# One transformer block in float32 on one core: where VectorE makes the weight sums of the up projection, who scales the keys, and how the first gate's row is made

## The chip, the cores and the metric

The kernel runs on one core of one Trainium2 chip. The metric is the device time of one execution in microseconds (us). Before the change the median of three runs was 2684.64 us (2683.98 to 2686.53).

## The reference

One block of a network on 512 tokens of width D = 2048, with 256 context tokens, all in float32:

```python
sh1, sc1, g1, sh2, sc2, g2 = split(silu(c) @ w_ada + b_ada, 6)      # the same for the context
px = modulate(x, sh1, sc1) @ w_in                                   # q, v, two forget gates, g, pool, conv
pc = modulate(ctx, csh1, csc1) @ w_in[:, :4 * 1024]
_, s_f, s_b = hgrn2_bidir(pc, ...)                                  # states left by the context
ox, _, _ = hgrn2_bidir(px, ..., s_f, s_b, True)                     # 8 heads of 128, forward and backward
yx = concatenate([ox, local_mixers(px[..., 5120:])], -1) @ w_out
x = layer_norm(ALPHA * x + g1 * yx, ln1_g, ln1_b)
u, g = split(modulate(x, sh2, sc2) @ w_up, 2)                       # 2 x 5632 columns
x = layer_norm(ALPHA * x + g2 * ((u * silu(dwconv3(g))) @ w_down), ln2_g, ln2_b)
```

`hgrn2_bidir` is a gated linear attention: each token's key and value enter a state that a forget gate shrinks, once in each direction.

## The kernel before

**Products.** TensorE works on a rounded float32 format. Each operand is therefore split into a high part (a cast, on ScalarE) and a low part (the value less its high part, on VectorE), and each product is three matmuls: high by high, high by low, low by high (`mm3`, lines L111, L112, L113 in turn; tiles named `h` or `H` are high, `l` or `L` low). `wload` (L95 to L106) does this for a streamed weight: a transfer on SyncE's queue into `wr`, the cast (L105), the subtraction (L106), with three buffers for the raw tile and two for each part.

**Stages.** The ramp (`ada_first`, `modulate1`, `ramp`) computes the first modulation, transposes the normalised tokens and the context (`hxh`/`hxl` at L310/L311, `hch`/`hcl` at L329/L330), and projects the context and the first heads. It lasts to about 391 us. Then `pair`, `conv` and `pool` project the tokens on all columns of `w_in`, to about 1024 us. Between two weight tiles of a projection they call `background()` (L645), which steps two generators of the linear attention (`gla`, L551, one for each of two heads) and three steps of `ada_rest` (L658), which streams the rest of `w_ada` and sums it on VectorE (`aacc`, L680 and L682).

A `gla` generator does one level of a binary tree over the tokens at each step (`LEVELS` = 1 to 64): it copies keys (`kc`, ScalarE, L562), multiplies keys by queries on TensorE (`lv`, L566), puts the masked result into `A` (VectorE, L641), scales the queries (`Q`, VectorE, L582) and the keys (`K`, two GpSimd operations, L585 and L586), and multiplies the decays (`T`, VectorE, L587). At the first level it also adds the keys of both directions (`kd`, GpSimd, L572) for the diagonal (`dg`, TensorE).

From 1024 to 1225 us `out_half` (L815) multiplies by `w_out`, once for each half of the tokens, in four blocks `j` of 512 columns, each from eight weight tiles. `norm_mid` (L846) does the layer norms behind it and transposes the tokens for the feed-forward part (`x2T`). The gate g1 lies as a column over the partitions (`mods2`), but is needed as a row on all partitions: `row_prepare` (L708) makes four diagonal matrices (`dg`, L715), their high part `dh` (L718) and low part `dl` (L719); `row_chunk` (L722) multiplies each by a matrix of ones (`row_g`, L726 and L727) and copies the result (`rowt_g`, L729). The product with the gate is L840 (`wt`).

**The up projection.** Two pairs of column groups are done plainly (`up_half`). The other twenty (`up_pair`, L1032; from 1333.62 to about 2176 us) use the seven-product scheme of Strassen and Winograd on 2 x 2 blocks (`combine`, `up_block`). One call of `weights7` (L977), a block here, loads four tiles of 128 rows by four column tiles into `W` (SyncE, L989), makes the three further factors of the scheme by sums on VectorE (L992, L993, L994: 128 x 1024, 128 x 512 and 128 x 512 elements), and has `parts` (L968) split it in two units: cast `H` (L973) and low part `L` (L974), each 128 x 1792. A unit feeds 42 matmuls of 256 columns, a block 84. A pair has a gate `g` and a value `u`, each of two blocks (`_0` and `_1`), so there are 80 blocks. After a gate's or value's last block VectorE adds up the products (`Z`, L1026 to L1029) and does the convolution and the gating (`cv`, L936, L938, L1042, L1047).

**What sets the order.** The engines run their queues in order. A scheduler places what the program traces, by priority: weights are traced under `high_priority(offset=AHEAD)`, so that they are placed ahead of the work around them, as far as data and buffers allow. There are three buffers of `W` (two in `ww`, one in `w3`), and three each of `H` and `L`. So the transfer into a block's `W` waits until the last low part of the block three before has been made, and a unit's cast waits until TensorE has used the unit three before.

**The rest.** `down` (L1104, about 2176 to 2627 us) multiplies by `w_down`; `finish` does the last layer norm.

Of the kernel before, what the change touches and what calls it, by code (L numbers as in the profile page):

```python
# [16 lines left out]
P = 128  # L17
# [55 lines left out]
class Kernel:  # L73
# [35 lines left out]
    def mm3(self, out, st, mv, start, stop):  # L109
        mm = self.nc.tensor.matmul  # L110
        mm(out=out, lhsT=st[0], rhs=mv[0], start=start, stop=False)  # L111
        mm(out=out, lhsT=st[0], rhs=mv[1], start=False, stop=False)  # L112
        mm(out=out, lhsT=st[1], rhs=mv[0], start=False, stop=stop)  # L113
# [21 lines left out]
    def setup(self):  # L135
        nc, I, pp = self.nc, self.I, self.persist
        self.ident = pp.tile([P, P], F32, name="ident")
        make_identity(nc, self.ident)
        self.ones = pp.tile([P, 32], F32, name="ones")
        nc.vector.memset(self.ones, 1.0)  # L140
        self.ones_r = pp.tile([P, P], F32R, name="ones_r")
        nc.scalar.copy(out=self.ones_r, in_=vw(self.ones[:, :], [[0, 4], [1, 32]]))
        self.mhalf = pp.tile([P, 4], F32, name="mhalf")
        nc.vector.memset(self.mhalf, -0.5)
        self.zero = pp.tile([P, 1], F32, name="zero")
        nc.vector.memset(self.zero, 0.0)
        self.cols = {}
# [149 lines left out]
    def modulate1(self, xp, rp, k0, n):  # L297

        nc = self.nc
        m = lambda k, i: self.mods1[:, 4 * k + i:4 * k + i + 1]  # L300
        tmp = xp.tile([P, n, L], F32, name=f"tx_{k0}", tag="v", bufs=2)
        for e in range(n):
            k = k0 + e
            fs = slice((k % 4) * P, (k % 4 + 1) * P)
            pt = self.glbank(f"xT_{k}")
            for t in range(NTT):
                nc.tensor.transpose(out=pt[:, t * P:(t + 1) * P], in_=self.xn[t][k // 4][:, fs], identity=self.ident)
            nc.vector.tensor_scalar(out=tmp[:, e], in0=pt, scalar1=m(k, 2), scalar2=m(k, 0), op0=ALU.mult, op1=ALU.add)
            h, l = self.a2(f"hxh_{k}"), self.a2(f"hxl_{k}")
            nc.scalar.copy(out=h, in_=tmp[:, e])  # L310
            (nc.vector if k0 < 2 else nc.gpsimd).tensor_tensor(out=l, in0=tmp[:, e], in1=h.bitcast(F32), op=ALU.subtract)  # L311
            self.hxh.append(h)
            self.hxl.append(l)

    def modulate1_ctx(self, rp, k0, n):
# [14 lines left out]
        nc.gpsimd.tensor_tensor(out=l, in0=tmp, in1=h.bitcast(F32), op=ALU.subtract)  # L330
# [5 lines left out]
    def proj_T(self, banks, wt, kts, hi, lo, first, last, shared=False):  # L336

        wh, wl = wt
        for j, k in enumerate(kts):
            for h in range(2):  # L340
                self.mm3(banks[h], (wh[:, j, h * P:(h + 1) * P], wl[:, j, h * P:(h + 1) * P]),
                         (hi[k], lo[k]),
                         start=(first and j == 0 and (h == 0 or not shared)),
                         stop=(last and j == len(kts) - 1 and (h == 1 or not shared)))

    def proj_N(self, banks, wt, kts, hi, lo, ntt, first, last):

        wh, wl = wt
        for j, k in enumerate(kts):
            for t in range(ntt):  # L350
                tk = slice(t * P, (t + 1) * P)
                self.mm3(banks[t // 2][:, (t % 2) * 256:(t % 2) * 256 + 256],
                         (hi[k][:, tk], lo[k][:, tk]), (wh[:, j, :], wl[:, j, :]),
                         start=(first and j == 0 and t % 2 == 0),
                         stop=(last and j == len(kts) - 1 and t % 2 == 1))
# [195 lines left out]
    def gla(self, gp, hd, q, Q, K, T, V, gs):  # L551
# [7 lines left out]
        for li, m in enumerate(LEVELS):  # L559
# [8 lines left out]
            if li == 0:  # L568
# [3 lines left out]
                nc.gpsimd.tensor_tensor(out=kd, in0=K[:, 0], in1=K[:, 1], op=ALU.add)  # L572
# [10 lines left out]
            kf = vw(Ka, [[2 * m, nb], [1, m]])  # L583
            kb = vw(Ka, [[2 * m, nb], [1, m]], L + m)
            nc.gpsimd.tensor_tensor(out=kf, in0=kf, in1=vw(cur, [[2, nb], [0, m]], ts_ + 1), op=ALU.mult)  # L585
            nc.gpsimd.tensor_tensor(out=kb, in0=kb, in1=vw(cur, [[2, nb], [0, m]]), op=ALU.mult)  # L586
# [58 lines left out]
    def background(self):  # L645
# [3 lines left out]
        if self.steps:  # L649
            next(self.steps[0], None)  # L650
            if n < len(LEVELS) or n >= len(LEVELS) + TAIL_LAG:
                next(self.steps[1], None)
# [54 lines left out]

    def row_prepare(self, name, base, j, dg=None):  # L708

        nc = self.nc  # L710
        if dg is None:
            dg = self.a2(f"dg_{name}_{j}", F32)
        dh, dl = self.a2(f"dh_{name}_{j}"), self.a2(f"dl_{name}_{j}")
        for i in range(4):
            nc.vector.tensor_scalar(out=dg[:, i * P:(i + 1) * P], in0=self.ident,  # L715
                                    scalar1=self.mods2[:, base + 4 * j + i:base + 4 * j + i + 1], scalar2=None,
                                    op0=ALU.mult)
        nc.scalar.copy(out=dh, in_=dg)  # L718
        nc.vector.tensor_tensor(out=dl, in0=dg, in1=dh.bitcast(F32), op=ALU.subtract)  # L719
        return dh, dl  # L720

    def row_chunk(self, pool, name, j, parts, tag):  # L722

        nc = self.nc
        pb = self.glbank(f"row_{name}_{j}")
        nc.tensor.matmul(out=pb, lhsT=self.ones_r, rhs=parts[0], start=True, stop=False)  # L726
        nc.tensor.matmul(out=pb, lhsT=self.ones_r, rhs=parts[1], start=False, stop=True)  # L727
        t = pool.tile([P, 512], F32, name=f"rowt_{name}_{j}", tag=tag[0], bufs=tag[1])
        nc.scalar.copy(out=t, in_=pb)  # L729
        return t  # L730
# [84 lines left out]
    def out_half(self, cp, hf):  # L815
# [8 lines left out]
        for j in range(4):  # L824
            b = [self.mmbank(f"wo_{hf}_{j}_{i}") for i in range(2)]
            for q in range(8):
                if q == 4:
                    parts = self.row_prepare(f"g1_{hf}", 0, j,
                                             cp.tile([P, 512], F32, name=f"dg_{hf}_{j}", tag="rc", bufs=2))
# [7 lines left out]
            g1 = self.row_chunk(cp, f"g1_{hf}", j, parts, ("rb", 1))  # L837
# [130 lines left out]
    def parts(self, ww, name, src, n):  # L968
# [5 lines left out]
        nc.vector.tensor_tensor(out=Lw[:, 0:n], in0=src, in1=H[:, 0:n].bitcast(F32), op=ALU.subtract)  # L974
        return H, Lw

    def weights7(self, ww, name, src, c0):  # L977
# [6 lines left out]
        with self.tc.high_priority(offset=AHEAD):  # L984
# [7 lines left out]
            tt(out=pair(4, 3), in0=pair(3, 1), in1=pair(2, 3), op=ALU.subtract)  # L992
            tt(out=W[:, :, 5], in0=W[:, :, 1], in1=W[:, :, 4], op=ALU.subtract)  # L993
            tt(out=W[:, :, 6], in0=W[:, :, 0], in1=W[:, :, 5], op=ALU.subtract)  # L994
            units = []
            for c in range(0, NB, NU):
                units += self.parts(ww, f"{name}_{c}", W[:, c:c + NU].rearrange("p a s m -> p (a s m)"), 7 * NU * P),
        return units
# [179 lines left out]
    def run(self):  # L1178
# [5 lines left out]
        self.y_d = [self.dram.tile([P, 4, 512], F32, name=f"y_d{t}") for t in range(NTT)]  # L1184
        self.g2_d = self.dram.tile([1, D], F32, name="g2_d")
        self.y, self.h2, self.S, self.h = {}, ({}, {}), {}, {}
        self.upc = self.wcount = 0
        with tc.tile_pool(name="wts", bufs=1, reuse_waits="tile", side="right") as self.wts:
# [77 lines left out]
```

## Time and profile before

| | |
|---|---|
| median of three runs | 2684.64 us |
| profiled execution, its own time | 2687.12 us |
| its span | 2685.3 us |
| mean granted TensorE clock | 0.985 |
| busy: TensorE, VectorE, ScalarE, GpSimd | 2545.6, 1897.1, 928.8, 256.1 us |
| up projection | 1333.62 to about 2176 us |

The profile is of one execution. The span reaches from its first to its last instruction, and the execution's own time is 1.8 us longer. Busy times are shares of that span; an average over the stages says little, since the ramp, the projections, the up and the down projection have different limits. A row of a group names line, engine, operation, the tile written and the tiles read, the count, the busy time in us and the mean of one in ns, and then the idle time of the engine just ahead, with what ended it. A wait's row has the total in us, the count and the longest. A row of the timeline has start and length in us, and in brackets the idle time before it.

### The profile page before, as it was taken

To read this page: it belongs to the slowest core of one execution; us is meant where nothing else is said; L and a number is where in the kernel's file an instruction comes from. 1 tells how busy PE (TensorE), PEld (TensorE's weight loads), DVE (VectorE), ACT (ScalarE), POOL (GpSimd) and SP (SyncE) were. 2 spreads that over 40 slices of the span, in tenths; PEclk is the share of its full clock that TensorE was granted. 3 is DMA by queue.
4 is the path that set the end of the run, shared out by engine and by line. 5 is a ranking of instruction groups with operands and counts; after the bars stand their busy time and mean duration, and the time that the engine had idled before them with its cause. 6 is when DMAs were issued, how large, how long until landed. Compare 5 with 4: busy or idle time off the path is not lost.

```text
span 2685.3 us, 40002 instructions
## 1 busy us (share of the span) xinstructions
PE 2545.6 (95%) x16332; PEld 2240.9 (83%) x16332; DVE 1897.1 (71%) x2408; ACT 928.8 (35%) x1119; POOL 256.1 (10%) x255
## 2 busy tenths in 40 slices
PE   5999999999999999999899999999999899999996
PEld 4677998888878888769899999999999888888885
DVE  5543569968698866778988889888898864433338
ACT  5221254232333324354543334433343342222111
POOL 0120102213051300001100000000000000000005
PEclk9999999999999999999999999999999999999998
DMA  8755236756646546657533333333333374333321
GB/s 266 235 181 164 87 95 224 235 167 197 204 148 209 160 128 207 209 188 243 160 111 120 109 110 118 111 107 117 116 104 125 103 247 155 127 122 131 109 94 63
DMA packets 301461, 409.85 MB, mean 153 GB/s; under 512 B 17669, under 2 KB 193117, under 8 KB 300765
## 3 DMA queue, kind: packets, MB, share of 16 engines
q1 hardware_dynamic: 297692, 395.76, 45.8%
q0 software_dynamic: 3584, 11.54, 1.1%
q8 instruction: 128, 2.10, 0.4%
q14 instruction: 57, 0.46, 0.1%
HBM read 387.30 MB, written 19.93 MB: 152 GB/s over the span
## 4 chain that ended last, share of the span: by engine, by line
PE 55%; DVE 19%; DMA 15%; issue 6%; ACT 2%; POOL 1%; SPq 1%; DVEq 0%; POOLq 0%; ACTq 0%
DMA W_g<-in_w_up_dram 7%; DMA W_u<-in_w_up_dram 6%; PE dn L113 6%; PE dn L112 6%; PE dn L111 5%; DVE L_g L974 3%; DVE L_u L974 3%; DVE W_u L992 2%; PE wo L112 2%; PE wo L113 2%; PE wo L111 1%; PE rx L111 1%; PE rc L111 1%; PE rx L113 1%; PE rc L112 1%
## 5 line engine op out<-in xcount | busy, mean ns | idle before, releaser
L974 DVE TENSOR_TENSOR L_dn<-W_dn,H_dn 128x1536 fp32r<-128x1536 f32 (+1 forms) x56 | 96.2, 1719 | 223.2 <-ACT H_dn L973 223.2
L973 ACT CAST H_u<-W_u 128x1792 fp32r<-128x1792 f32 x80 | 135.6, 1695 | 174.1 <-PE ub_g L112 171.9
L682 DVE SCALAR_TENSOR_TENSOR aacc<-a,csil,aacc 128x512 f32<-128x512 f32 x240 | 188.7, 787 | 8.3 <-DMA a<-in_w_ada_dram 3.2
L113 PE MATMUL dn<-H_dn,hl 128*128 128x512 f32 x480 | 188.6, 394 | 0.0
L112 PE MATMUL dn<-L_dn,hh 128*128 128x512 f32 x480 | 188.2, 392 | 0.0
L111 PE MATMUL dn<-H_dn,hh 128*128 128x512 f32 x480 | 185.9, 388 | 0.0
L973 ACT CAST H_dn<-W_dn 128x1536 fp32r<-128x1536 f32 (+1 forms) x56 | 81.4, 1453 | 294.9 <-PE dn L113 290.3
L974 DVE TENSOR_TENSOR L_u<-W_u,H_u 128x1792 fp32r<-128x1792 f32 x80 | 161.5, 2018 | 2.5 <-ACT H_u L973 2.5
L974 DVE TENSOR_TENSOR L_g<-W_g,H_g 128x1792 fp32r<-128x1792 f32 x80 | 161.4, 2018 | 1.0 <-ACT H_g L973 1.0
L973 ACT CAST H_g<-W_g 128x1792 fp32r<-128x1792 f32 x80 | 135.0, 1689 | 75.8 <-PE ub_g L112 55.7
L113 PE MATMUL ub_g<-h2h,L_g 128*128 128x256 f32 x480 | 137.8, 288 | 23.8 <-DVE L_g L974 23.3
L113 PE MATMUL ub_u<-h2h,L_u 128*128 128x256 f32 x480 | 136.3, 284 | 22.4 <-DVE L_u L974 22.4
L111 PE MATMUL ub_g<-h2h,H_g 128*128 128x256 f32 x480 | 134.6, 280 | 8.5 <-ACT H_g L973 8.5
L112 PE MATMUL ub_g<-h2l,H_g 128*128 128x256 f32 x480 | 134.4, 280 | 0.0
L112 PE MATMUL ub_u<-h2l,H_u 128*128 128x256 f32 x480 | 132.9, 277 | 0.0
L111 PE MATMUL ub_u<-h2h,H_u 128*128 128x256 f32 x480 | 132.8, 277 | 0.0
L105 ACT CAST wh_r<-wr_r 128x1024 fp32r<-128x1024 f32 x48 | 50.3, 1048 | 208.1 <-PE rc L113 112.4
L113 PEld LDWEIGHTS ub_g<-h2h,L_g 128*128 128x128 f32 x480 | 91.6, 191 | 29.4 <-DVE L_g L974 29.1
L113 PEld LDWEIGHTS ub_u<-h2h,L_u 128*128 128x128 f32 x480 | 90.2, 188 | 28.3 <-DVE L_u L974 28.3
L106 DVE TENSOR_TENSOR wl_wo<-wr_wo,wh_wo 128x1024 fp32r<-128x1024 f32 x64 | 78.3, 1223 | 50.0 <-ACT wh_wo L105 49.9
L112 PEld LDWEIGHTS dn<-L_dn,hh 128*128 128x128 f32 x480 | 90.1, 188 | 21.4 <-DVE L_dn L974 0.4
L992 DVE TENSOR_TENSOR W_g<-W_g 128x1024 f32<-128x1024 f32 x40 | 49.0, 1225 | 82.9 <-DMA W_g<-in_w_up_dram 82.7
(447 smaller groups left out, 8360.9 us busy)
## 6 DMA issues: line engine op xcount, KB each, us to landing
a<-in_w_ada_dram SPq DMA_DIRECT2D x256, 256.0 KB, 3.8
W_g<-in_w_up_dram SPq DMA_DIRECT2D x80, 512.0 KB, 5.4
W_u<-in_w_up_dram SPq DMA_DIRECT2D x80, 512.0 KB, 3.9
W_dn<-in_w_down_dram SPq DMA_DIRECT2D x24, 1536.0 KB, 6.7
wr_wo<-in_w_out_dram SPq DMA_DIRECT2D x64, 512.0 KB, 4.6
ada<-in_w_ada_dram SPq DMA_DIRECT2D x56, 512.0 KB, 5.0
wr_r<-in_w_in_dram SPq DMA_DIRECT2D x48, 512.0 KB, 3.7
wr_up<-in_w_up_dram SPq DMA_DIRECT2D x32, 512.0 KB, 4.5
```

What stands on the lines that cost most here:

```text
L105: nc.scalar.copy(out=hi, in_=raw)
L106: (lo_engine or nc.vector).tensor_tensor(out=lo, in0=raw, in1=hi.bitcast(F32), op=ALU.subtract)
L111: mm(out=out, lhsT=st[0], rhs=mv[0], start=start, stop=False)
L112: mm(out=out, lhsT=st[0], rhs=mv[1], start=False, stop=False)
L113: mm(out=out, lhsT=st[1], rhs=mv[0], start=False, stop=stop)
L682: nc.vector.scalar_tensor_tensor(out=acc, in0=raw, scalar=self.csil[:, k:k + 1], in1=acc, op0=ALU.mult, op1=ALU.add)
L973: nc.scalar.copy(out=H[:, 0:n], in_=src)
L974: nc.vector.tensor_tensor(out=Lw[:, 0:n], in0=src, in1=H[:, 0:n].bitcast(F32), op=ALU.subtract)
L992: tt(out=pair(4, 3), in0=pair(3, 1), in1=pair(2, 3), op=ALU.subtract)
```

## The change

1. **Sums of the up projection.** `weights7` puts its three sums into `issue_after(self.low_first.ins)`: on VectorE they are queued behind the low part of the first unit of the block traced before. This is an order in the queue alone, with no wait. `parts` keeps its last low part as `self.low` for that.
2. **Keys of the linear attention.** The two GpSimd operations on `K` become one VectorE operation on both directions, and the addition `kd` goes to VectorE too.
3. **The levels' place.** `background()` queues what the two `gla` generators issue behind the projection matmul last traced (`self.last_mm`, kept by `proj_T` and `proj_N`).
4. **Low parts of the ramp.** `hxl` (14 of 16) and `hcl` (9) go from GpSimd to VectorE.
5. **The first gate's row.** `row_prepare` and `row_chunk` go, and the matrix of ones. `ada_columns` writes g1 from `mods2` to DRAM once (`g1_d`, 2048 elements), and `out_half` loads each 512 columns of it, broadcast to 128 partitions, by SyncE's queue at the fifth of the eight weight tiles: eight loads into one buffer.

```diff
@@ mm3 @@
-        mm(out=out, lhsT=st[1], rhs=mv[0], start=False, stop=stop)
+        return mm(out=out, lhsT=st[1], rhs=mv[0], start=False, stop=stop)
@@ setup @@
-        self.ones_r = pp.tile([P, P], F32R, name="ones_r")
-        nc.scalar.copy(out=self.ones_r, in_=vw(self.ones[:, :], [[0, 4], [1, 32]]))
@@ modulate1 @@
-            (nc.vector if k0 < 2 else nc.gpsimd).tensor_tensor(out=l, in0=tmp[:, e], in1=h.bitcast(F32), op=ALU.subtract)
+            nc.vector.tensor_tensor(out=l, in0=tmp[:, e], in1=h.bitcast(F32), op=ALU.subtract)
@@ modulate1_ctx @@
-        nc.gpsimd.tensor_tensor(out=l, in0=tmp, in1=h.bitcast(F32), op=ALU.subtract)
+        nc.vector.tensor_tensor(out=l, in0=tmp, in1=h.bitcast(F32), op=ALU.subtract)
@@ proj_T, and proj_N in the same way @@
-                self.mm3(banks[h], ...
+                self.last_mm = self.mm3(banks[h], ...
@@ gla @@
-                nc.gpsimd.tensor_tensor(out=kd, in0=K[:, 0], in1=K[:, 1], op=ALU.add)
+                nc.vector.tensor_tensor(out=kd, in0=K[:, 0], in1=K[:, 1], op=ALU.add)
...
-            kf = vw(Ka, [[2 * m, nb], [1, m]])
-            kb = vw(Ka, [[2 * m, nb], [1, m]], L + m)
-            nc.gpsimd.tensor_tensor(out=kf, in0=kf, in1=vw(cur, [[2, nb], [0, m]], ts_ + 1), op=ALU.mult)
-            nc.gpsimd.tensor_tensor(out=kb, in0=kb, in1=vw(cur, [[2, nb], [0, m]]), op=ALU.mult)
+            kv = vw(Ka, [[L + m, 2], [2 * m, nb], [1, m]])
+            nc.vector.tensor_tensor(out=kv, in0=kv, in1=vw(cur, [[-ts_ - 1, 2], [2, nb], [0, m]], ts_ + 1), op=ALU.mult)
@@ background @@
-            next(self.steps[0], None)
-            if n < len(LEVELS) or n >= len(LEVELS) + TAIL_LAG:
-                next(self.steps[1], None)
+            with self.tc.issue_after(self.last_mm.ins):
+                next(self.steps[0], None)
+                if n < len(LEVELS) or n >= len(LEVELS) + TAIL_LAG:
+                    next(self.steps[1], None)
@@ ada_columns; row_prepare and row_chunk are removed @@
+        if g == 3:
+            nc.sync.dma_start(out=self.g1_d.rearrange("o (k p) -> (o p) k", p=P), in_=self.mods2[:, 0:KT])
@@ out_half @@
                 if q == 4:
-                    parts = self.row_prepare(f"g1_{hf}", 0, j,
-                                             cp.tile([P, 512], F32, name=f"dg_{hf}_{j}", tag="rc", bufs=2))
+                    g1 = cp.tile([P, 512], F32, name=f"g1_{hf}_{j}", tag="rb", bufs=1)
+                    nc.sync.dma_start(out=g1, in_=self.g1_d[0:1, 512 * j:512 * j + 512].broadcast_to((P, 512)))
...
-            g1 = self.row_chunk(cp, f"g1_{hf}", j, parts, ("rb", 1))
@@ parts @@
-        nc.vector.tensor_tensor(out=Lw[:, 0:n], in0=src, in1=H[:, 0:n].bitcast(F32), op=ALU.subtract)
+        self.low = nc.vector.tensor_tensor(out=Lw[:, 0:n], in0=src, in1=H[:, 0:n].bitcast(F32), op=ALU.subtract)
@@ weights7 @@
-            tt(out=pair(4, 3), in0=pair(3, 1), in1=pair(2, 3), op=ALU.subtract)
-            tt(out=W[:, :, 5], in0=W[:, :, 1], in1=W[:, :, 4], op=ALU.subtract)
-            tt(out=W[:, :, 6], in0=W[:, :, 0], in1=W[:, :, 5], op=ALU.subtract)
+            with self.tc.issue_after(self.low_first.ins) if self.low_first else nullcontext():
+                tt(out=pair(4, 3), in0=pair(3, 1), in1=pair(2, 3), op=ALU.subtract)
+                tt(out=W[:, :, 5], in0=W[:, :, 1], in1=W[:, :, 4], op=ALU.subtract)
+                tt(out=W[:, :, 6], in0=W[:, :, 0], in1=W[:, :, 5], op=ALU.subtract)
             units = []
             for c in range(0, NB, NU):
                 units += self.parts(ww, f"{name}_{c}", ...
+                if c == 0:
+                    self.low_first = self.low
@@ run @@
+        self.g1_d = self.dram.tile([1, D], F32, name="g1_d")
...
+        self.low_first = None
```

More of the change, by code (lines that the diff above doesn't have):

```diff
@@ L1 @@
-from contextlib import ExitStack
+from contextlib import ExitStack, nullcontext
 import numpy as np
@@ L340, in proj_T @@
             for h in range(2):
[L341 to L344, printed above, removed]
+                self.last_mm = self.mm3(banks[h], (wh[:, j, h * P:(h + 1) * P], wl[:, j, h * P:(h + 1) * P]),
+                                       (hi[k], lo[k]),
+                                       start=(first and j == 0 and (h == 0 or not shared)),
+                                       stop=(last and j == len(kts) - 1 and (h == 1 or not shared)))
     def proj_N(self, banks, wt, kts, hi, lo, ntt, first, last):
@@ L351, in proj_N @@
                 tk = slice(t * P, (t + 1) * P)
[L352 to L355, printed above, removed]
+                self.last_mm = self.mm3(banks[t // 2][:, (t % 2) * 256:(t % 2) * 256 + 256],
+                                       (hi[k][:, tk], lo[k][:, tk]), (wh[:, j, :], wl[:, j, :]),
+                                       start=(first and j == 0 and t % 2 == 0),
+                                       stop=(last and j == len(kts) - 1 and t % 2 == 1))
     def ramp(self, xp, rp):
@@ L706, in ada_columns @@
             nc.vector.tensor_tensor(out=dst, in0=pc[:, 0:4], in1=bc, op=ALU.add)
[L708 to L730, printed above, removed]
+        if g == 3:
+            nc.sync.dma_start(out=self.g1_d.rearrange("o (k p) -> (o p) k", p=P), in_=self.mods2[:, 0:KT])
     def local_setup(self, gp):
```

## The prediction

> **What bounds the kernel now.** I read the chain of waits of the page first, to see which engines carry the end, then the waits, the stages by windows, and the chain in order of time inside the longest stage. The page's chain:
>
> ```profile
> PE 55%; DVE 19%; DMA 15%; issue 6%; ACT 2%; POOL 1%; SPq 1%; DVEq 0%; POOLq 0%; ACTq 0%
> ```
>
> TensorE carries a little over half; VectorE and transfers carry a third. The windows (columns: length; busy time and count of PE, PEld, DVE, ACT, POOL; granted TensorE clock; DMA share; GB/s) say where TensorE isn't the limit:
>
> ```profile
> 1333.00:2176.00 843.00, 796.19 (x6720) 784.71 (x6721) 709.93 (x718) 336.21 (x285) 20.81 (x38) 0.98 0.35 115
> 455.00:1030.00 575.00, 565.24 (x3143) 479.00 (x3142) 461.06 (x688) 184.42 (x317) 133.80 (x126) 1.00 0.57 178
> 2300.00:2400.00 100.00, 100.00 (x439) 82.05 (x438) 43.20 (x49) 25.79 (x26) 0.00 (x0) 1.00 0.40 135
> ```
>
> The first is the up projection (80 blocks of 84 matmuls, hence x6720), the second the projections with the linear attention beside them, the third a piece of the down projection, where TensorE never stops. The up projection idles 47 us, at a mean clock of 0.98. Its waits (us in total, times, longest):
>
> ```profile
> DVE W_g L992 <- DMA W_g<-in_w_up_dram: 82.7, 37, 4.7
> DVE W_u L992 <- DMA W_u<-in_w_up_dram: 33.6, 25, 3.1
> PE ub_g L113 <- DVE L_g L974: 23.3, 18, 2.9
> PE ub_u L113 <- DVE L_u L974: 22.4, 30, 2.8
> ```
>
> TensorE waits for low parts L, and VectorE, which makes them, waits 116 us for weights. The chain near 1605 us shows how they hang together:
>
> ```profile
> 1602.93 5.33 DMA W_g<-in_w_up_dram
> 1608.38 1.24 DVE W_g L992
> ...
> 1610.97 2.03 DVE L_u L974
> ...
> 1613.43 4.83 DMA W_g<-in_w_up_dram
> ...
> 1621.49 1.94 DVE L_u L974
> ```
>
> A loop: the last low part of one block frees a weight tile; its transfer takes about 5 us; VectorE stands at the sums of the tile that lands (L992 to L994); behind those sums, in VectorE's order, stands the next block's last low part, which frees the next tile. The loop turns in 1613.43 − 1602.93 = 10.5 us a block. TensorE alone would need less:
>
> ```profile
> 1607.20 0.28 PE L111 MATMUL ub_u<-h2h,H_u 128*128 128x256 f32 x1
> 1611.96 0.28 PE L111 MATMUL ub_u<-h2h,H_u 128*128 128x256 f32 x1
> 1613.04 0.38 PE L113 MATMUL ub_u<-h2h,L_u 128*128 128x256 f32 x1 [0.69 <-DVE L_u L974]
> ```
>
> 42 matmuls lie between the first two rows: 4.76 us, 0.1133 us each, 9.52 us a block, and 6720 of them 761.4 us.
>
> **The sums' place on VectorE** (the largest part). Before, VectorE's order in the sixth of the twenty pairs (L974 a low part, L992 to L994 the sums, `_0` and `_1` a gate's or value's two blocks, the last digit of L the unit):
>
> ```order
> L974 TENSOR_TENSOR L_g_0_0_14188<-W_g_0_14181,H_g_0_0_14187 128x1792
> L1042 TENSOR_TENSOR cv_13959<-cv_13959,cs_13960 128x512
> L992 TENSOR_TENSOR W_u_0_14402<-W_u_0_14402 128x4x2x128
> L993 TENSOR_TENSOR W_u_0_14402<-W_u_0_14402 128x4x128
> L994 TENSOR_TENSOR W_u_0_14402<-W_u_0_14402 128x4x128
> L974 TENSOR_TENSOR L_g_0_2_14192<-W_g_0_14181,H_g_0_2_14191 128x1792
> ```
>
> The changed kernel at the same pair (L948 a low part, L968 to L970 the sums):
>
> ```order
> L948 TENSOR_TENSOR L_g_0_0_14036<-W_g_0_14029,H_g_0_0_14035 128x1792
> L968 TENSOR_TENSOR W_g_1_14127<-W_g_1_14127 128x4x2x128
> L1020 TENSOR_TENSOR cv_13807<-cv_13807,cs_13808 128x512
> L969 TENSOR_TENSOR W_g_1_14127<-W_g_1_14127 128x4x128
> L970 TENSOR_TENSOR W_g_1_14127<-W_g_1_14127 128x4x128
> L948 TENSOR_TENSOR L_g_0_2_14040<-W_g_0_14029,H_g_0_2_14039 128x1792
> ```
>
> Between a block's two low parts stood the sums of the block two on (`W_u_0` in `g_0`); now stand those of the next block (`W_g_1`). Nothing is added; each sum comes a block later. The tile that VectorE stands at was therefore freed a whole block earlier: its transfer, 4.83 to 5.33 us, has a block's 9.5 us more to land in, and the loop opens. What is late next? VectorE's own work: 709.93 us over 80 blocks is 8.87 us a block, under 9.52. One new wait: a block's first high part (ScalarE, L973) needs its sums, and the low part needs that cast.
>
> ```profile
> 1607.33 1.70 ACT L973 CAST H_u<-W_u 128x1792 fp32r<-128x1792 f32 x1 [1.60 <-PE ub_g L112]
> 1608.38 1.23 DVE L992 TENSOR_TENSOR W_g<-W_g 128x1024 f32<-128x1024 f32 x1 [3.35 <-DMA W_g<-in_w_up_dram]
> 1609.64 0.69 DVE L993 TENSOR_TENSOR W_g<-W_g 128x512 f32<-128x512 f32 x1
> 1610.36 0.69 DVE L994 TENSOR_TENSOR W_g<-W_g 128x512 f32<-128x512 f32 x1
> ```
>
> Where other VectorE work stands between the last sum and the low part, the cast's 1.70 us is covered; in the order of a whole pair it stands bare once in four blocks (the last sum of `u_0` right before the low part of `u_0`). Four blocks then take VectorE 4 x 8.87 + 1.70 = 37.2 us against TensorE's 38.1: still TensorE, by 0.9 us. By my estimate from these durations, laid out in the new order, each low part is then ready 4 to 7 us before its matmul.
>
> The price: the stage's TensorE time runs from 1333.62 to about 2176, 842.4 us, against 761.4: 81 us above its matmuls. Of these 45.7 are the two waits for L above; the mean clock of 0.98 is worth about 0.02 x 843 = 17; the rest is slow restarts (0.38 us for 0.28) and gaps too short for a row. The first matmuls keep a share:
>
> ```profile
> 1337.96 0.58 PE L113 MATMUL ub_g<-h2h,L_g 128*128 128x256 f32 x1 [2.26 <-DVE L_g L974]
> 1767.81 0.58 PE L113 MATMUL ub_g<-h2h,L_g 128*128 128x256 f32 x1 [2.69 <-DVE L_g L974]
> 1767.00:1774.00 7.00, 6.19 (x29) 6.19 (x30) 3.29 (x3) 0.37 (x1) 0.55 (x1) 0.51 0.59 189
> ```
>
> At 1337.96 the stage starts at double-length matmuls (0.58), which the change doesn't cure; I leave 11 us for the start and for odd waits and take **−70 us**; bounds −45 (the named waits alone) and −78. After 1767.81 the clock is 0.51 for 7 us, behind a wait of 2.69 us: the slow stretches follow waits, and I let them go with the waits. The Trainium skill ("TensorE: Matmul & The Clock Gate", section "HAM oscillation") asks only for no idle gap of TensorE above about 3.4 us; by that rule a 2.69 us wait should not slow the clock, and the stretches would stay. The trace speaks against it in this place; its price is among the rivals.
>
> **The first gate's row** (output projection). Removed per half and column block: 4 VectorE diagonals, a cast, a subtraction, 2 matmuls, a ScalarE copy. On TensorE that is 16 matmuls:
>
> ```profile
> 1184.17 0.39 PE L112 MATMUL wo<-wl_wo,oh 128*128 128x512 f32 x1
> 1185.98 0.39 PE L111 MATMUL wo<-wh_wo,oh 128*128 128x512 f32 x1
> PE row_g L726 <- ACT dh_g L718: 4.3, 2, 3.9
> PE wo L111 <- DVE wt L840: 1.4, 1, 1.4
> 1173.00:1184.00 11.00, 7.74 (x18) 5.47 (x19) 7.23 (x12) 4.65 (x8) 0.00 (x0) 0.53 0.17 69
> ```
>
> Eight steps in 1.81 us: 0.226 each, 16 of them 3.6 us. The row's wait is 4.3 us, that for the product behind it 1.4, and the clock of 0.53 over the 11 us that follow costs 0.47 x 11 = 5.2. Together 14.5. The product (L840) still stands behind low parts of the normalised tokens on VectorE, so part of the wait stays: **−12 us**. In its place come 8 broadcast loads on SyncE's queue. Where one stands, of the changed kernel (`g_0_1` the row, `wr_wo` weights):
>
> ```order
> L100 DMA wr_wo_1_3_9290<-in_w_out_dram 128x2x512
> L804 DMA g_0_1_9308<-g_d 128x512
> L797 DMA y_9888<-in_x_dram 128x2048
> L100 DMA wr_wo_1_4_9310<-in_w_out_dram 128x2x512
> L100 DMA wr_wo_1_5_9328<-in_w_out_dram 128x2x512
> ```
>
> The row has one buffer, so this load waits until the last block's product has been read, with `wr_wo_1_4` queued behind it. Nearest rows for a broadcast load and for the one write that feeds it (KB, us to landing):
>
> ```profile
> ln_g<-in_ln_g_dram SPq DMA_DIRECT2D x12, 256.0 KB, 4.7
> g_d<-mods SPq DMA_DIRECT2D x1, 8.0 KB, 11.0
> ```
>
> The read is issued half a column block (some 11 us: 48 matmuls) ahead of its use, so 4.7 us is covered, and the weights behind it have buffers ahead. At worst three loads a half come 4.7 us late, +28 less the 14.5: bounds −14.5 and +14. The write's 11.0 us lies far ahead of any reader.
>
> **The level work of the linear attention.** Two GpSimd operations per head and level become one of VectorE, and the levels' matmuls queue behind the projection matmul last traced. Grouped rows of 440 to 1035 us, and two transfers' low parts beside and without GpSimd work:
>
> ```profile
> L586 POOL TENSOR_TENSOR K<-K,T 128x256 f32<-128x256 f32 x55 | 60.7, 1105 | 3.2 <-DVE T L484 3.2
> L585 POOL TENSOR_TENSOR K<-K,T 128x256 f32<-128x256 f32 x55 | 57.7, 1049 | 66.5 <-ACT kc L562 49.1 <-DVE T L587 11.6 <-DVE T L484 5.4
> L582 DVE TENSOR_TENSOR Q<-Q,T 128x512 f32<-128x512 f32 x56 | 50.9, 915 | 0.0
> 464.12 1.69 DVE L106 TENSOR_TENSOR wl_x_q<-wr_x_q,wh_x_q 128x1024 fp32r<-128x1024 f32 x1
> 481.59 1.21 DVE L106 TENSOR_TENSOR wl_x_v<-wr_x_v,wh_x_v 128x1024 fp32r<-128x1024 f32 x1
> ```
>
> VectorE's order at level 32 in the changed kernel (L582 the new operation, L580 the old one on Q, L583 the decays):
>
> ```order
> L582 TENSOR_TENSOR K_4082<-K_4082,T_0_4117 128x2x8x32
> L583 TENSOR_TENSOR T_267<-T_0_4117 128x2x8
> L582 TENSOR_TENSOR K_4083<-K_4083,T_1_4138 128x2x8x32
> L583 TENSOR_TENSOR T_268<-T_1_4138 128x2x8
> L679 SCALAR_TENSOR_TENSOR aacc_4289<-a_2_7_4509,csil,aacc_4289 128x512
> ```
>
> VectorE takes on 56 operations of 128x512 and 8 additions: 64 x 0.69 (L993's row, the same shape) to 64 x 0.915 (Q's mean, beside GpSimd), 44 to 59 us. It gets back what GpSimd's presence stretched: 56 x (0.915 − 0.69) = 13 on Q, and 0.48 on each low part caught like that at 464.12. VectorE then has 461 + 44 − 15 = 490 of 575 us, still below TensorE's 565, and a head's keys are scaled 1.05 + 1.10 − 0.69 = 1.5 us sooner. TensorE idles 9.8 us here; I take **−6 us**, bounds −10 and +15 (a late level here and there).
>
> **The ramp.** 23 low parts go from GpSimd to VectorE:
>
> ```profile
> L311 POOL TENSOR_TENSOR hxl<-tx,hxh 128x512 fp32r<-128x512 f32 x14 | 20.8, 1517 | 144.4 <-ACT hxh L310 144.4
> ```
>
> 1.52 us becomes about 0.69, half as late for its matmul, and VectorE has room: 0, bounds ±3.
>
> **The sum.** −70 − 12 − 6 = −88 us. The profiled execution took 2687.1 us, span 2685.3; it becomes 2599. The median of the runs, 2684.64, lies 2.5 lower: **2597 us**.
>
> **The rivals.**
> *The transfers stay the last wait* (the moved sums wait as before; nothing gained in the up projection): for it, 116 us of waits that the change makes no shorter by itself; against it, the order above, a block of lead against a 5.4 us landing. Then −12 − 6: 2667. Chance 0.05.
> *VectorE close behind takes over the up projection*: if the cast stands bare in three blocks of four and not in one, four take 4 x 8.87 + 3 x 1.70 = 40.6 us against 38.1, and 80 take 812; with the start's 5 us 817 for 842, −25, less 18 elsewhere: 2644. For it, the thin 0.9 us of lead; against it, other work of VectorE between. Chance 0.10.
> *Slow clock stretches stay without waits*: if something else than the waits sets them, 12 of the 17 us return (5 lie at the start and are kept anyway): −58, less 18 elsewhere: 2611. Chance 0.07. This is the rival that follows from the Trainium skill's limit of about 3.4 us for an idle gap (the section named above), which no wait of the stage reaches.
> *VectorE bound in the level work*: if VectorE ends last in the stretches with a level, the whole 44 us of its new work lies on the path, in place of the −6: −70 − 12 + 44 = −38, 2649. It needs VectorE near 565 us there; the sum is 490, and 520 with nothing given back. Chance 0.08.
> *Slower: sum, cast and low part become one bare chain.* If VectorE waits for the 1.70 us cast at both units of every block, a block takes 8.87 + 2 x 1.70 = 12.3 us, 80 take 982: +139, less 18: +121, 2808. It decides from 1.1 bare casts a block on (8.87 + 1.1 x 1.70 = 10.75, which eats the other gains too). For it, the sums now come just ahead of their use; against it, the second unit's sums are the first's, already done, and in three blocks of four other work stands before the first. Chance 0.05.
> That the sums don't move is excluded by the order.
>
> **How the numbers follow.** The forecast itself has 0.65 (2573 to 2625). The slow stretches, the close VectorE and part of the bound level work lie within 2573 to 2645; the transfers, the slower case, the rest of the level work and a little below are left out: 0.2. A measurement of this kernel tells 0.2%, 5.4 us, from no change. Faster: all but the slower case and what of the bad ends meets (a bound level work with late loads and transfers): 0.92; same 0.02; slower 0.06.
>
> **What would show it.** Right: waits of VectorE for W_g and W_u nearly gone, TensorE's waits for L under 10 us, four blocks in about 38.1 us, clock 1.00 from 1350 on, no `row_g`, GpSimd idle between 455 and 1030, VectorE some 490 us there. Wrong: VectorE waiting for H casts in the up projection, TensorE's waits for L unchanged, or `lv` waits above 20 us.

## The result and the profile after

The changed kernel took 2603.35 us (median of four runs, 2599.65 to 2630.36), against 2684.41 us (four runs): a ratio of 0.9718, 95% interval 0.9653 to 0.9783. The profiled execution took 2599.65 us, with a span of 2597.8. Of the four runs three lie between 2599.65 and 2604.57 and one at 2630.36; executions of that second kind recur below, and two profiles fell on one (of the row by matrices of ones, and of the changed kernel again), whose up projection is left out of the comparisons of stages. Four executions among the runs below, of 3086 to 6482 us at mean granted clocks of 0.44 to 0.77, are left out of every time and ratio.

The page's busy times and its chain of waits, after:

```profile
PE 2510.2 (97%) x16316; PEld 2219.3 (85%) x16316; DVE 1891.9 (73%) x2455; ACT 927.9 (36%) x1101; POOL 93.3 (4%) x112
PE 87%; DVE 5%; DMA 4%; ACT 1%; issue 1%; POOL 1%; SPq 0%; DVEq 0%; POOLq 0%; ACTq 0%
```

TensorE now carries 87% of the chain, where it was 55%. The windows (columns as in the prediction) of the up projection, a piece of it, and the projections with the linear attention:

```profile
1323.00:2088.00 765.00, 764.43 (x6718) 764.15 (x6719) 705.01 (x718) 345.88 (x285) 20.74 (x38) 1.00 0.39 127
1600.00:1700.00 100.00, 100.00 (x885) 100.00 (x884) 91.76 (x94) 45.34 (x37) 2.87 (x6) 1.00 0.39 125
455.00:1030.00 575.00, 566.19 (x3153) 482.51 (x3153) 463.55 (x746) 184.42 (x316) 12.07 (x12) 0.99 0.58 179
```

In the up projection TensorE doesn't stop, at full clock. Its first row and the first of the down projection give the stage's length:

```profile
1323.57 0.58 PE L111 MATMUL ub_g<-h2h,H_g 128*128 128x256 f32 x1 [8.47 <-ACT H_g L947]
2088.28 0.39 PE L111 MATMUL dn<-H_dn,hh 128*128 128x512 f32 x1
```

764.7 us from the first gate matmul to the first down matmul, 842.4 before. In the waits, VectorE's waits for `W_g` and `W_u` and TensorE's waits for low parts have no row any more. What is left in the stage:

```profile
DVE L_u L948 <- ACT H_u L947: 38.0, 20, 2.2
DVE Z_g L1004 <- PE ub_g L113: 7.3, 17, 0.5
PE ub_g L111 <- ACT H_g L947: 8.5, 1, 8.5
DVE L_g L948 <- ACT H_g L947: 3.6, 2, 1.8
```

The first row is the bare cast: 20 times, once in four blocks, 1.9 us each (the last row adds two at the stage's start). It looks like this on VectorE (the last sum of `u_0`, then the low part that waits for the cast of what the sum made):

```profile
1716.49 0.69 DVE L970 TENSOR_TENSOR W_u<-W_u 128x512 f32<-128x512 f32 x1
1719.06 2.02 DVE L948 TENSOR_TENSOR L_u<-W_u,H_u 128x1792 fp32r<-128x1792 f32 x1 [1.89 <-ACT H_u L947]
```

Stage by stage, from the first matmul of each to that of the next, in us:

| from the first matmul of | before | after |
|---|---|---|
| (start) to `px_q`: the ramp | 391.1 | 391.3 |
| `px_q`: projections and linear attention | 632.6 | 630.9 |
| `wo`: output projection | 199.9 | 187.5 |
| `up`: the two plain up pairs | 110.0 | 113.9 |
| `ub_g`: the seven-product up projection | 842.4 | 764.7 |
| `dn`: down (to `fin`, the last layer norm) | 450.7 | 450.7 |

So 77.7 us came from the sums' place, 12.4 from the output projection, 1.7 from the linear attention, and 3.9 went back in the plain up pairs. The linear attention no longer waits for its levels, but lost almost as much in one place. SyncE's queue, VectorE and TensorE there (start, length, then in brackets the idle time before):

```profile
571.34 0.38 SPq L705 DMA_DIRECT2D g_d<-mods  x1
```
```profile
578.32 0.75 DVE L679 SCALAR_TENSOR_TENSOR aacc<-a,csil,aacc 128x512 f32<-128x512 f32 x1 [2.25 <-DMA a<-in_w_ada_dram]
585.72 0.75 DVE L679 SCALAR_TENSOR_TENSOR aacc<-a,csil,aacc 128x512 f32<-128x512 f32 x1 [6.65 <-DMA a<-in_w_ada_dram]
```
```profile
587.66 0.79 PE L113 MATMUL px_f<-hxh,wl_x_f 128*128 128x512 f32 x1 [5.46 <-DVE wl_x_f L106]
```
```profile
g_d<-mods SPq DMA_DIRECT2D x1, 8.0 KB, 10.9
```

The write of g1, 2048 pieces of four bytes, is issued at 571.34 and lands 10.9 us later. The loads of `w_ada` issued behind it come late, VectorE stands at the sum that needs them for 2.25 and 6.65 us, and behind that sum in VectorE's queue is the low part of a weight for which TensorE then waits 5.46 us. The clock falls to about a half after that (0.53 from 585 to 592).

### The profile page after: what moved, and what is told of

Its sections match the earlier page's. It is cut to its first block, busy times and chain, and to the rows that moved or that the text cites. A ratio compares the mean times of both kernels' runs of the same rounds, so it can differ in the third digit from the quotient of the medians.

```text
span 2597.8 us, 39767 instructions
## 1 busy us (share of the span) xinstructions
PE 2510.2 (97%) x16316; PEld 2219.3 (85%) x16316; DVE 1891.9 (73%) x2455; ACT 927.9 (36%) x1101; POOL 93.3 (4%) x112
## 4 chain that ended last, share of the span: by engine, by line
PE 87%; DVE 5%; DMA 4%; ACT 1%; issue 1%; POOL 1%; SPq 0%; DVEq 0%; POOLq 0%; ACTq 0%
PE dn L113 6%; PE dn L112 6%; PE dn L111 6%; PE ub_g L111 5%; PE ub_g L113 5%; PE ub_g L112 5%; PE ub_u L111 5%; PE ub_u L113 5%; PE ub_u L112 5%; PE lv L564 2%; PE ada L278 2%; PE rc L111 2%; PE rx L111 2%; PE rc L113 2%; PE rc L112 2%; PE rx L113 2%
## 5 line engine op out<-in xcount | busy, mean ns | idle before, releaser
L679 DVE SCALAR_TENSOR_TENSOR aacc<-a,csil,aacc 128x512 f32<-128x512 f32 x240 | 179.5, 749 | 19.2 <-DMA a<-in_w_ada_dram 14.7
L111 PEld LDWEIGHTS dn<-H_dn,hh 128*128 128x128 f32 x480 | 90.1, 188 | 20.1
L105 ACT CAST wh_wo<-wr_wo 128x1024 fp32r<-128x1024 f32 x64 | 67.4, 1053 | 108.7 <-PE wo L113 89.9
L112 PE MATMUL wo<-wl_wo,oh 128*128 128x512 f32 x256 | 101.6, 397 | 4.7 <-DVE wl_wo L106 4.2
```

Source lines behind the costliest of these rows:

```text
L105: nc.scalar.copy(out=hi, in_=raw)
L679: nc.vector.scalar_tensor_tensor(out=acc, in0=raw, scalar=self.csil[:, k:k + 1], in1=acc, op0=ALU.mult, op1=ALU.add)
```

## The experiments

Times are medians, and each ratio is to runs of the kernel before on the same chip. Dots mark what is left out of an edit.

**The sums alone** (kernel before, with the change to `parts` and `weights7` only).

```diff
+            with self.tc.issue_after(self.low_first.ins) if self.low_first else nullcontext():
                 tt(out=pair(4, 3), in0=pair(3, 1), in1=pair(2, 3), op=ALU.subtract)
...
+                if c == 0:
+                    self.low_first = self.low
```

> The kernel before with the sums of the up projection alone in their new place; nothing else of the change. Theory (the moved sums open the loop of transfer, sums and last low part; the other parts give about 10 us): the stage from the first gate matmul to the first down matmul, 842.4 us before and 764.7 in the changed kernel, takes 763 to 768 us here, and the time falls by 74 to 80 us, to about 2607. Rival (the gain comes from VectorE and GpSimd no longer disturbing each other, or from the earlier start, and the sums' place alone does part of it): the stage stays above 790 us and the time above 2630.

Measured: 2612.41 us against 2689.6, ratio 0.971 (0.9694 to 0.9726); the stage takes 764.0 us, and TensorE runs without a gap:

```profile
1400.00:2000.00 600.00, 600.00 (x5296) 600.00 (x5296) 557.64 (x572) 270.60 (x222) 17.44 (x32) 1.00 0.38 125
```

The sums' place alone makes the whole gain of the up projection. The rival falls: GpSimd does its old work in this kernel.

**Weights loaded twice** (the changed kernel; the second load of the same tiles goes into the same buffer).

```diff
+            for _ in range(2):
-            for r0, s0 in ((c0, 2), (c0 + KT // 2, 0)):
+                for r0, s0 in ((c0, 2), (c0 + KT // 2, 0)):
...
```

> The changed kernel, but each block of the up projection loads its four weight tiles twice into the same buffer, the second load behind the first. Theory (the transfer has about a block, 9.5 us, of lead, of which it uses 4.6): a second load of 4 to 5 us still fits or nearly so; the up projection grows by 0 to 25 us. Rival (the transfer is hidden by little and is again the last wait as soon as it takes longer): each block grows by some 4 us, the stage by 200 us or more.

Measured: 2608.98 us (ratio 0.9699, 0.9684 to 0.9715), the stage 763.9 us. The same window, at twice the bytes:

```profile
1400.00:2000.00 600.00, 600.00 (x5296) 600.00 (x5296) 556.45 (x569) 269.08 (x219) 17.52 (x32) 1.00 0.76 237
```

The DMA share doubles from 0.38 to 0.76 and not one matmul is late: the transfers have at least the time of a second load in hand. The 6 us or so that the whole kernel lost lie ahead of the stage (113.9 became 123.6 us from the first plain up matmul). TensorE's wait for the stage's first cast, 8.5 us in the changed kernel, is 15.5 here:

```profile
PE ub_g L111 <- ACT H_g L947: 15.5, 1, 15.5
```

**VectorE's margin** (the changed kernel; the last of the three sums made once, or three times, more in each block).

```diff
+                for _ in range(1):
+                    tt(out=W[:, :, 6], in0=W[:, :, 0], in1=W[:, :, 5], op=ALU.subtract)
```

> The changed kernel with one more VectorE operation of 128 x 512 in each block of the up projection (the last sum made twice). VectorE has 705 us of work in the stage's 765, 8.8 a block against TensorE's 9.53. Theory (TensorE is the bound with some 0.7 us to spare, less 0.4 for the bare cast once in four blocks): one operation more, 0.62 to 0.69 us, makes 9.4 to 9.5, plus 0.4: 9.85 against 9.53, so the stage grows by 0 to 30 us. Rival (VectorE has room, the bare cast is covered): below 3 us.

> The same with three more VectorE operations in each block. Theory: 8.8 + 3 x 0.65 + 0.4 = 11.2 us a block, VectorE the bound, the stage 890 to 900 us, the time higher by 110 to 145 us than the changed kernel. Rival (VectorE not near the bound): the time rises by less than 60 us.

Measured: 2665.45 us with one (ratio 0.992, 0.9895 to 0.9946), 2802.64 with three (1.0423, 1.0395 to 1.0452). The stage takes 821.3 and 953.8 us, 57 and 189 more than in the changed kernel, where I had expected at most 30 and 135. The stage with one, a piece of it, and its waits:

```profile
1326.00:2147.00 821.00, 793.10 (x6716) 779.15 (x6717) 740.91 (x793) 328.23 (x283) 20.81 (x38) 1.00 0.36 118
1400.00:2000.00 600.00, 577.65 (x4913) 566.67 (x4911) 543.56 (x587) 236.39 (x203) 16.41 (x30) 1.00 0.36 116
```
```profile
DVE L_u L948 <- ACT H_u L947: 61.1, 39, 2.2
DVE L_g L948 <- ACT H_g L947: 14.5, 21, 1.8
PE ub_g L113 <- DVE L_g L948: 18.7, 35, 0.9
```

VectorE is the bound, together with the casts that it stands for: the bare cast now stands at 39 + 21 = 60 low parts in place of 22. That is the case of the rival *VectorE close behind*: it is one operation away. VectorE's busy time in the stage is 36 us longer (740.9 against 705.0) and its waits for casts are 34 us longer (61.1 + 14.5 against 38.0 + 3.6), 70 in all, of which the stage shows 57. The other 13 are, as an estimate, what VectorE had to spare. Read back into the changed kernel it comes out alike: 705.0 us of work and 38.0 + 7.3 + 3.6 of waits are 754 of the stage's 764.7 us, which leaves some 11 us, 0.13 a block. The added operation stood between the sums and the cast that needs them; what it costs elsewhere in VectorE's order wasn't tried.

**The row by matrices of ones** (the changed kernel with `row_prepare` and `row_chunk` back, without `g1_d`).

```diff
-                    g1 = cp.tile([P, 512], F32, name=f"g1_{hf}_{j}", tag="rb", bufs=1)
-                    nc.sync.dma_start(out=g1, in_=self.g1_d[...].broadcast_to((P, 512)))
+                    parts = self.row_prepare(f"g1_{hf}", 0, j, cp.tile(...))
...
+            g1 = self.row_chunk(cp, f"g1_{hf}", j, parts, ("rb", 1))
```

> The changed kernel with the first gate's row made by matrices of ones again, and so without the write to DRAM and the eight loads. Theory (the row's loads save 12 us at the output projection, but the one write of 2048 single elements, at 571 us, holds up the loads queued behind it and costs TensorE a wait of 5.6 us and a stretch of half clock, some 9 us): the time rises by only 2 to 5 us against the changed kernel; the wait of px_f for wl_x_f (5.5 us) and the slow stretch at 585 to 592 us are gone, and the output projection is 11 to 13 us longer. Rival (the wait near 580 us has another cause, such as the levels' new place): it stays, and the time rises by 11 to 13 us.

Measured: 2600.26 us (ratio 0.9694, 0.9634 to 0.9753; three runs at 2598.79 to 2601.65, one at 2630.25). The projections take 624.0 us (6.9 less than in the changed kernel), the output projection 199.1 (11.6 more), the plain up pairs 110.5 (3.4 less). The wait of `px_f` has no row. Part five of the change, as it stands, gains nothing that I can tell: 11.6 − 6.9 − 3.4 = 1.3 us.

**g1 transposed before it is written** (the changed kernel).

```diff
-            nc.sync.dma_start(out=self.g1_d.rearrange("o (k p) -> (o p) k", p=P), in_=self.mods2[:, 0:KT])
+            pt = self.glbank("g1T")
+            nc.tensor.transpose(out=pt[0:KT, 0:P], in_=self.mods2[:, 0:KT], identity=self.ident)
+            gt = self.a2("g1t", F32)
+            nc.scalar.copy(out=gt[0:KT, 0:P], in_=pt[0:KT, 0:P])
+            nc.sync.dma_start(out=self.g1_d.rearrange("o (k p) -> (o k) p", p=P), in_=gt[0:KT, 0:P])
```

> The changed kernel, but g1 is transposed on TensorE to 16 rows of 128 before it is written to DRAM, so that the write has 16 pieces of 512 bytes in place of 2048 of 4. Theory (the small pieces of the write hold up the loads behind it): the write lands in 2 to 5 us in place of 11.7, VectorE's wait of 6.6 us for a piece of w_ada at 586 us goes, and the time falls by 7 to 10 us, to about 2591. Rival (the loads there are late for a reason of their own): the wait stays, the time moves by less than 2 us.

Measured: 2592.47 us (2591.38 to 2598.45; ratio 0.9643, 0.9624 to 0.9663), the shortest median of all. The projections take 622.8 us, 8.1 less. The write's row, and VectorE's wait for `w_ada`:

```profile
g_d<-g1t SPq DMA_DIRECT2D x1, 8.0 KB, 2.1
```
```profile
DVE aacc L679 <- DMA a<-in_w_ada_dram: 4.3, 6, 1.5
```

The same 8 KB in 16 pieces land in 2.1 us, and the long waits are gone (the longest is 1.5 us). This shows the cause of the lost 8 us.

**The keys back on GpSimd, and the levels as before** (two kernels, each the changed kernel with one edit undone).

```diff
-            kv = vw(Ka, [[L + m, 2], [2 * m, nb], [1, m]])
-            nc.vector.tensor_tensor(out=kv, in0=kv, in1=..., op=ALU.mult)
+            nc.gpsimd.tensor_tensor(out=kf, in0=kf, in1=..., op=ALU.mult)
+            nc.gpsimd.tensor_tensor(out=kb, in0=kb, in1=..., op=ALU.mult)
```

> The changed kernel with the keys' scaling and the keys' addition back on GpSimd; the levels' new place stays. Theory (the sooner keys did it): lv waits of 5 to 13 us return and the time rises by 4 to 12 us, while VectorE's busy time from 455 to 1030 us falls by only some 0 to 10 us, since Q and the low parts get longer again beside GpSimd (Q from 0.74 to 0.9 us). Rival (the place did it): the time moves by less than 3 us. By full blocking, the Trainium skill's (SBUF — State Buffer, section Who interferes with whom) reading, Q's mean would rise to well above 1.2 us.

```diff
-            with self.tc.issue_after(self.last_mm.ins):
-                next(self.steps[0], None)
...
+            next(self.steps[0], None)
...
```

> The changed kernel without the levels' new place: the two generators of the linear attention are issued as before, and not behind the last projection matmul. Theory (the lv waits went because keys are scaled sooner on VectorE; the place matters little): TensorE's waits for lv stay under 4 us in all, and the time moves by less than 3 us. Rival (the place in the queue did it): 8 to 13 us of lv waits return, and the time rises by as much.

Measured: with the keys on GpSimd 2610.38 us (ratio 0.9709, 0.9687 to 0.973), projections 639.9 us, 9.0 more than in the changed kernel. With the levels as before 2602 to 2604 us in two runs and 2630.59 in a third (ratio 0.9714, 0.9657 to 0.9771), projections 628.6 us, 2.3 less. TensorE's waits for `lv` have no row in the changed kernel, nor with the levels as before. The largest in the kernel before:

```profile
PE lv L566 <- DVE Q L544: 3.1, 4, 1.1
PE lv L566 <- DVE Q L582: 2.8, 4, 1.1
```

With the keys on GpSimd they are back, 7.0 us in all, the largest being

```profile
PE lv L564 <- DVE Q L542: 3.1, 4, 1.1
PE lv L564 <- ACT kc L560: 1.6, 1, 1.6
PE lv L564 <- DVE Q L580: 1.2, 3, 0.6
```

So the keys' move did it, not the levels' place, which without the keys' move doesn't keep the waits away, and with it does nothing that can be told. That it did so by scaling the keys sooner, as I had expected, is not shown. Only 1.6 of the 7.0 us name the copy of the keys (`kc`); 4.3 name Q, which is VectorE's own work. One of the longest, 1.1 us at 605 us, comes behind these two rows, the first of VectorE, the second of GpSimd (the addition `kd`):

```profile
601.28 1.59 DVE L480 TENSOR_SCALAR T<-T,lb_oml,lb_lo 128x512 f32<-128x512 f32 x1
601.29 1.29 POOL L570 TENSOR_TENSOR kd<-K 128x512 f32<-128x512 f32 x1 [46.34 <-ACT K L485]
```

In the changed kernel, where `kd` is VectorE's, the same operation on T takes 0.54 us. VectorE held up beside GpSimd accounts for a wait like this one; how the whole gain divides between that and the sooner keys stays open. The groups of Q, and the window, with the keys on GpSimd:

```profile
L580 DVE TENSOR_TENSOR Q<-Q,T 128x512 f32<-128x512 f32 x56 | 52.6, 944 | 0.0
```
```profile
455.00:1030.00 575.00, 562.02 (x3115) 476.77 (x3116) 455.54 (x678) 180.68 (x311) 133.37 (x126) 0.99 0.57 175
```

In the changed kernel Q and the new operation on K read

```profile
L580 DVE TENSOR_TENSOR Q<-Q,T 128x512 f32<-128x512 f32 x56 | 41.4, 740 | 0.0
L582 DVE TENSOR_TENSOR K<-K,T 128x512 f32<-128x512 f32 x55 | 37.4, 682 | 0.0
```

Moving 55 operations of 682 ns, and the additions, to VectorE raised its busy time by only 463.55 − 455.54 = 8 us, since it gets 11.2 us back on Q alone. The mean of 944 ns hides two kinds of Q. Rows of GpSimd and VectorE, with the keys on GpSimd:

```profile
491.28 0.62 POOL L583 TENSOR_TENSOR K<-K,T 128x256 f32<-128x256 f32 x1
491.39 1.06 DVE L580 TENSOR_TENSOR Q<-Q,T 128x512 f32<-128x512 f32 x1
493.00 0.68 DVE L580 TENSOR_TENSOR Q<-Q,T 128x512 f32<-128x512 f32 x1
```

The first Q starts while GpSimd works on K, and ends 0.55 us after that work has ended (491.90); the second meets no GpSimd operation. Of the 56, 23 meet none and take 0.67 to 0.69 us; 24 start with one under way that has more than 0.25 us to go, of which 16 end 0.55 us behind its end, and seven 1.00 to 1.03, all of the first level, where Q takes 1.10 to 1.15 us in the changed kernel too. So Q waits until GpSimd's operation is done. This is the exclusive lock of which the Trainium skill speaks ("SBUF — State Buffer", section "Who interferes with whom"), and the trace agrees with it. That Q's mean stayed below the 1.2 us that I had put for full blocking is no evidence against it: fewer than half of the Q's run into a GpSimd operation, and one on K takes 0.61 us alone.

**Both, and the loads' queue.** The transposed row with the levels as before (both edits as above), and the transposed row with its eight loads on GpSimd's queue:

```diff
-                    nc.sync.dma_start(out=g1, in_=self.g1_d[0:1, 512 * j:512 * j + 512].broadcast_to((P, 512)))
+                    nc.gpsimd.dma_start(out=g1, in_=self.g1_d[0:1, 512 * j:512 * j + 512].broadcast_to((P, 512)))
```

> The changed kernel with g1 transposed before it is written to DRAM, and the levels of the linear attention issued as before the change. Theory (the levels' place costs 2 us, as the run without it alone showed: 628.6 us from the first q matmul to the first output matmul against 630.9; the small pieces cost 8): the two add, the stretch takes 619 to 622 us, the time is 2587 to 2592 us, the shortest of all. Rival (once the write is out of the way, the two are the same): within 2 us of the kernel with the transposed row alone, 2591 to 2593.

> The changed kernel with g1 transposed before it is written, and the eight loads of the row issued from GpSimd's queue in place of SyncE's. Theory (the plain up projections behind the output projection lose 4 to 7 us because VectorE stands there for the layer norm's rows, whose loads come late behind SyncE's other loads; the row's loads are part of that): 2 to 4 us of the 6.9 come back, the stretch from the first plain up matmul to the first gate matmul takes 112 to 115 us against 116.9. Rival (the layer norm's rows are late because the output projection itself ends sooner, with the same bytes in less time): no change, 116 to 118 us.

Measured: 2593.78 us (ratio 0.9656, 0.9638 to 0.9674) and 2598.46 us (0.9708, 0.9667 to 0.9749; four runs at 2591 to 2601, two at 2622 and 2625). The first has 623.7 us of projections against 622.8 for the transposed row alone: no gain, my expectation missed. The second has 114.1 us in the plain up pairs, as I had expected, but so has the first, whose loads are on SyncE's queue. So this run tells nothing of the queue; the changed kernel's own two profiles give 113.9 and 117.8 for that stretch.

**The changed kernel again.**

> The changed kernel once more, unaltered, beside the two above on one chip. Theory: most executions at 2599 to 2605 us; one in four or so near 2630, with the up projection's matmuls at 0.118 us each in place of 0.113, as in one profile of the kernel with the row made by ones (30 us more in that stage alone). Rival (the 2630 us were chance of another kind): no execution above 2615.

Measured: 2616.93 us, with three runs at 2599.99 to 2605.30 and three at 2628.55 to 2633.08 (ratio 0.974, 0.9699 to 0.9782). With the first four runs, four of ten are of the second kind. A profile of each, the same 100 us of the up projection (the changed kernel's first, and this one):

```profile
1700.00:1800.00 100.00, 100.00 (x885) 100.00 (x884) 92.15 (x95) 43.81 (x35) 3.26 (x6) 1.00 0.39 129
```
```profile
1700.00:1800.00 100.00, 100.00 (x851) 100.00 (x851) 90.43 (x93) 44.38 (x38) 2.18 (x4) 1.00 0.36 117
```

TensorE is busy all the time at full clock in both, but does 851 matmuls in place of 885.

## Why the prediction was right

**The sums' place** (−70, bounds −45 and −78; measured −77.7). The mechanism held in each step: the loop opened (no wait for a transfer left), TensorE became the bound at 9.52 us a block, the bare cast stood once in four blocks (20 times, and twice at the start). The term was too small by 8 us, since I kept 11 us for the start and odd waits; the stage needs 764.7 − 761.4 = 3.3 above its matmuls. The 8.47 us wait at its start lies outside that count, as it did before.

**The margin.** "Still TensorE, by 0.9 us" in four blocks: by the changed kernel's waits it is 11 us in 80 blocks, 0.5 in four. The step was right in sign. So was the estimate that low parts are ready 4 to 7 us before their matmul: the low part of the bare cast shown above ends at 1721.08, and its first matmul starts 5.7 us later; the median over the stage's 160 units is 5.5 us, 0.4 in the kernel before.

```profile
1726.74 0.28 PE L113 MATMUL ub_u<-h2h,L_u 128*128 128x256 f32 x1
```

But a lead is not spare work: with one more operation a block the same median is 2.3 us, and 72 of the 160 units have under 0.1.

**The output projection** (−12; measured −12.4 in the stage). Right there. But I had put the loads' cost at zero in the sum, and the plain up pairs behind it are 2 to 8 us longer in the nine profiles of kernels with these loads and single weight loads (113.9 to 117.8 us, against 110.0 to 112.1 in the three without). VectorE stands there for the layer norm's rows (`ln_g`, `ln_b`) 2.7 to 5.7 us in these nine, and 1.3 to 1.6 in the three. What of this is the loads, and what the earlier end of the output projection, stays open.

**The write of g1.** "The write's 11.0 us lies far ahead of any reader" is the sentence that failed. True of its reader, and beside the point: what counted was who is queued behind it. It cost 8 us, and took away most of the linear attention's gain.

**The linear attention** (−6; measured −1.7, and −9.8 with the write out of the way). The `lv` waits went, as forecast, and with the keys' move. The step forecast, keys scaled 1.5 us sooner, isn't shown: the waits that come back with the keys on GpSimd mostly name Q, which VectorE makes late where GpSimd holds it up. VectorE's load was sized wrong: 490 us forecast, 463.6 measured. The 15 us that I let GpSimd's absence give back were nearer 40.

**The ramp** (0; measured 0.2).

**The rivals.** The transfers as the last wait, and the slower chain, did not come: three blocks of four have cover. VectorE bound in the level work did not come either. The slow stretches went with the waits: none in the up projection from 1330 to its end. The Trainium skill's limit of about 3.4 us for an idle gap ("TensorE: Matmul & The Clock Gate", section "HAM oscillation") is too wide for this kernel: with three more VectorE operations in a block, stretches at half clock come back, behind waits of 2.1 us and less. By the trace's record of the clock there are 25 in that stage: eight begin behind one wait of 1.99 to 2.06 us, seventeen behind two of 0.69 to 1.38 us within 3.5 us.

```profile
1472.80 0.58 PE L113 MATMUL ub_g<-h2h,L_g 128*128 128x256 f32 x1 [2.06 <-DVE L_g L948]
```
```profile
1472.00:1476.00 4.00, 3.20 (x15) 3.20 (x16) 4.00 (x4) 0.00 (x0) 0.00 (x0) 0.60 0.04 8
```

The profiled execution came out 87.5 us shorter, against 88, by errors that cancelled: 8 too little in the up projection, 4 too much in the linear attention, 4 that were given back in the plain up pairs. That it came out so close is luck. The median of the runs is 2603.35 us against a forecast of 2597.

## What to carry to other kernels

Where an engine stands for a transfer and the transfer stands for that engine's own next work, ask what is queued between the two; an order of the queue alone, with no operation less, was worth 78 us of 2684. Before costing a transfer at nothing, look at the loads issued behind it, and at the size of its pieces. When a wait is taken away, add up work and waits of the engine that becomes second: here it has some 0.13 us a block left, and one more operation of 0.69 us a block, put ahead of a cast, lengthened the stage by 57 us.

## What the runs showed of the hardware

- A write of 8 KB in pieces of four bytes took 10.9 us and held up the loads behind it; in pieces of 512 bytes it took 2.1 us.
- The matmuls of the seven-product up projection have two speeds from one execution to the next, 0.113 and 0.118 us each, the same over all its 80 blocks (9.52 and 9.89 us) at a granted clock of 1.00. In the profile of the kernel with the row by ones the stage takes 794.3 us so, and 793.9 in the second one of the changed kernel. 80 x 0.37 = 30 us is nearly the whole difference between runs near 2600 and near 2630. The other stages' matmuls take the same in both. In the kernel before no execution stands apart so; a block there took 842.4/80 = 10.5 us, which may have covered it, but that isn't shown. What sets the speed, no run here shows.
- An operation of VectorE and one of GpSimd, each on two tiles, did not run side by side: Q, 0.68 us alone, took 1.04 to 1.17 where an operation on K was under way at its start, and ended 0.55 us after it.
